# Layer 0's per-layer embedding product at the start of a two-layer encoder kernel, its bias table's product first, and the table's eight skewed copies written one per block

## The chip, the cores and the metric

The kernel runs on 1 core of one Trainium2 chip. The metric is device microseconds of one execution; the times shown are the median of 3 runs with their lowest and highest. The profile is of one further execution. The granted TensorE clock of that execution was 0.989 of full speed on average.

## The reference, cut to what matters

The kernel computes two encoder layers on 1024 tokens of width 1024 in float32. Layer 0 mixes tokens by neighbourhood attention (16 heads), layer 1 by differential attention (8 heads) with a bias from a table of 32 buckets. Each layer ends with a gated per-layer embedding; `p[i]` and `ple_w_proj[i]` are inputs that depend on nothing computed before.

```python
def reference(x, p, norm_g, ...):
    for i in range(DEPTH):
        h = rms_norm(x, g[0])
        m = neighborhood_attention(...) if i % 2 == 0 else diff_attention(..., t5_table)
        x = x + rms_norm(m, g[1])
        f = conv_glu_ffn(rms_norm(x, g[2]), ...)
        x = x + rms_norm(f, g[3])
        gate = jax.nn.sigmoid(rms_norm(x, g[4]) @ ple_w_gate[i])
        x = x + gate * (p[i] @ ple_w_proj[i])
    return x
# inside diff_attention, for query positions qpos of a block:
#   bias = t5_table[t5_bucket(kpos[None, :] - qpos[:, None])]
```

## The kernel before, in words

**Products.** Every float32 operand of the large products is split into a high and a low part: ScalarE copies the rounded high part (L85), VectorE subtracts it from the source (L86). `mm3` (L104 to L109) then issues three matmuls of 128x128 by 128x512, high by high, high by low, low by high. `load_split` (L93) is the same with a load ahead of it into one of three `raw` pages.

**Order of the work.** PE's instructions stand in the order in which the program writes them. The other engines' order, and that of SP, whose queue issues every DMA, is set by the scheduler of the tile framework. Pages and banks are reused in turn; an instruction that needs a page waits for the last user of what lay there. SP's DMAs use eight completion lanes in turn: a DMA is issued only when the one eight places before it has landed.

**Start of layer 0.** `enter` (L1121) loads eight tiles of x, normalises each (square on ScalarE, L114, power on GpSimd, L119, product on VectorE, L127) and transposes them on PE (L135) into four `r1` pages, high and low parts for the two halves of the width. After four tiles it begins the first two projections on 256 columns (`begin`), and `mid` transposes the other four tiles between the steps of the queries' projection.

**Neighbourhood attention.** `qkv_stream` (L228) is a generator of projection steps, three matmuls each: for each of eight blocks of two heads the keys, the queries and the values. `na` (L441) runs 64 rounds of scores, softmax, transposes and values and takes some six steps of the generator in each round (`tick`). Block 0's projections run before the first round.

**Bias table of layer 1.** After block 0's queries `da_tables` (L480) multiplies the table of 32x8 by a one-hot matrix of 32x2047 in four matmuls (L491), writes the 8x2047 result to DRAM (L494) and issues eight DMAs from DRAM to DRAM (L500), each writing one head's row 128 times with a shift of one place, 1023.5 KB each. They are read in layer 1.

**Embedding product.** `embeddings` (L1099) splits the 256x1024 of p (transposed) and of `ple_w_proj`, and multiplies them: eight tiles of tokens, two halves, two steps of three matmuls, 96 matmuls of 512 columns; ScalarE copies each half to a page (L1118) and SP writes each tile to the DRAM tensor `pp` (L1119), which the end of the layer reads. Its 32 steps follow the last projection in the generator and so fill the last five rounds of attention, ahead of `first_out` (L651), which loads and splits the attention's output weight `na_w_o` and multiplies the first token tile by it (L637) in 14 steps. `mix_out` is the output stage that follows (L637 with `m`).

## Time and profile before

| | us |
|---|---|
| median of 3 runs (lowest, highest) | 2787.24 (2779.03, 2789.44) |
| profiled execution, its own time | 2781.16 |
| its span (first to last instruction) | 2779.2 |
| layer 0's embedding product, first to last matmul | 441.05 to 475.65 |
| the four matmuls of the bias table, first to the next product | 56.98 to 60.91 |
| the eight skewed copies, issue on SP | 64.11 to 69.24 |

A row of the timeline has the start in us, the length in us, the engine, the line, the operation, the tiles written and read (buffer numbers left out), their shapes, and in brackets the idle time of the engine before it with what ended it. A matmul's length holds its drain through the array, so the distance from one start to the next tells its pace. SPq is SP issuing DMAs; "DMA to landing" counts from the issue to the arrival. Of a table of stretches the columns are the stretch, its length, the busy time and count on PE, PE's weight loads, VectorE, ScalarE and GpSimd, the granted clock, the share of the 16 DMA engines that was busy, and GB/s.

### The profile page before, as it was taken

Reading aid. Unit: us, or ns where it says so; the run is one execution under the profiler, and the core shown is the slowest. Engines: PE = TensorE matmul, PEld = TensorE weight load, DVE = VectorE, ACT = ScalarE, POOL = GpSimd, SP = SyncE. Lnnn points to the kernel's source line nnn. Section 1 sums busy time; section 2 is a strip of 40 time slices with the busy share of each in tenths; the row PEclk is TensorE's granted clock in tenths of the full one; section 3 lists DMA queues with packets and bytes.
Section 4 is the critical chain, followed back from the end, with each engine's and each line's share of the span. In section 5 each row is a group of like instructions: output and inputs, shape, how many; then the busy total and the mean of one; then the engine's idle time right before and its main releaser. Section 6 shows DMA issues by size and latency. Waiting matters only on the chain.

```text
span 2779.2 us, 36486 instructions
## 1 busy us (share of the span) xinstructions
PE 2703.0 (97%) x13312; PEld 2257.8 (81%) x13312; DVE 1985.5 (71%) x3409; ACT 1344.3 (48%) x2491; POOL 498.3 (18%) x473
## 2 busy tenths in 40 slices
PE   7999999989999999999999999999989999999999
PEld 5788888867888888888888888887868888888887
DVE  5677776687777777666677777776687767777664
ACT  4555556443444435454455555566354444444452
POOL 2121220023334300001000000000033343300000
PEclk9999999999999999999999999999999999999999
DMA  6412214623222373343211111115413333272342
GB/s 183 169 52 67 64 49 158 166 71 106 106 96 104 108 266 117 106 143 115 98 45 45 45 46 45 38 38 179 138 64 114 103 103 114 94 285 93 116 149 98
DMA packets 129477, 298.48 MB, mean 107 GB/s; under 512 B 11753, under 2 KB 37737, under 8 KB 129297
## 3 DMA queue, kind: packets, MB, share of 16 engines
q1 hardware_dynamic: 129296, 296.15, 32.4%
q8 instruction: 104, 1.70, 0.3%
q14 instruction: 77, 0.62, 0.1%
HBM read 221.69 MB, written 86.61 MB: 111 GB/s over the span
## 4 chain that ended last, share of the span: by engine, by line
PE 87%; DMA 5%; DVE 4%; ACT 2%; issue 1%; POOL 0%; SPq 0%; ACTq 0%; DVEq 0%; POOLq 0%
PE b L107 20%; PE b L108 20%; PE b L109 20%; PE g L637 5%; PE m L637 5%; PE b L553 4%; PE s L515 2%; PE s L516 2%; PE b L539 2%; PE av L426 2%; PE b L135 2%; PE b L410 1%; DVE r L86 1%; DMA raw<-in_qkv 1%; DMA raw<-in_ple_w_gate 1%
## 5 line engine op out<-in xcount | busy, mean ns | idle before, releaser
L107 PE MATMUL b<-r,ws 128*128 128x512 f32 (+1 forms) x1328 | 549.3, 414 | 12.8 <-ACT r L85 9.5
L109 PE MATMUL b<-r,ws 128*128 128x512 f32 (+1 forms) x1328 | 521.0, 392 | 0.5 <-DVE ws L86 0.5
L108 PE MATMUL b<-r,ws 128*128 128x512 f32 (+1 forms) x1328 | 519.9, 391 | 1.0 <-DVE r L86 0.8
L107 PEld LDWEIGHTS b<-r,ws 128*128 128x128 f32 x1328 | 253.7, 191 | 59.4 <-ACT r L85 11.0
L109 PEld LDWEIGHTS b<-r,ws 128*128 128x128 f32 x1328 | 252.3, 190 | 54.0 <-DVE ws L86 1.0
L119 POOL TENSOR_TENSOR ss<-ss,mhalf 128x1 f32<-128x1 f32 x136 | 90.8, 669 | 1137.4 <-DVE ss L557 566.5
L368 ACT ACTIVATE E<-E,mn 128x1024 f32<-128x1024 f32 (+2 forms) x256 | 221.9, 867 | 147.5 <-DVE mn L364 145.1
L108 PEld LDWEIGHTS b<-r,ws 128*128 128x128 f32 x1328 | 254.2, 191 | 39.7 <-DVE r L86 3.3
L107 PE MATMUL b<-r,wa 128*128 128x512 f32 x688 | 268.6, 390 | 7.5 <-DVE v L906 7.5
L107 PE MATMUL b<-r,r 128*128 128x512 f32 x680 | 268.9, 395 | 4.0 <-DVE v L911 2.9
L108 PE MATMUL b<-r,wa 128*128 128x512 f32 x688 | 268.4, 390 | 0.0
L109 PE MATMUL b<-r,wa 128*128 128x512 f32 x688 | 268.3, 390 | 0.0
L109 PE MATMUL b<-r,r 128*128 128x512 f32 x680 | 265.2, 390 | 0.0
L108 PE MATMUL b<-r,r 128*128 128x512 f32 x680 | 265.2, 390 | 0.0
L86 DVE TENSOR_TENSOR r<-raw,r 128x512 fp32r<-128x512 f32 (+1 forms) x178 | 140.5, 795 | 110.9 <-ACT r L85 110.6
L85 ACT ACTIVATE r<-raw 128x512 fp32r<-128x512 f32 (+1 forms) x178 | 121.4, 689 | 198.7 <-PE b L108 161.6
L86 DVE TENSOR_TENSOR ws<-raw,ws 128x512 fp32r<-128x512 f32 (+3 forms) x168 | 157.6, 946 | 63.2 <-ACT ws L85 61.2
L85 ACT ACTIVATE ws<-raw 128x512 fp32r<-128x512 f32 (+3 forms) x168 | 124.6, 749 | 140.1 <-PE b L109 57.7
L364 DVE CUSTOM_DVE_ANT_0 E<-s,T 128x1024 f32<-128x1024 f32 x128 | 156.5, 1223 | 33.8 <-PE s L516 32.5
L107 PEld LDWEIGHTS b<-r,wa 128*128 128x128 f32 x688 | 129.7, 189 | 35.3 <-ACT cv L916 5.3
L637 PE MATMUL m<-r,ws 128*128 128x512 f32 x672 | 156.7, 392 | 0.0
L637 PE MATMUL g<-r,ws 128*128 128x512 f32 x672 | 155.9, 391 | 0.0
(182 smaller groups left out, 5336.4 us busy)
## 6 DMA issues: line engine op xcount, KB each, us to landing
raw<-in_w_in SPq DMA_DIRECT2D x86, 512.0 KB, 3.5
raw<-in_qkv SPq DMA_DIRECT2D x48, 512.0 KB, 5.6
spillS<-r SPq DMA_DIRECT2D x88, 256.0 KB, 2.7
r<-in_ffn_w_out SPq DMA_DIRECT2D x40, 512.0 KB, 10.1
raw<-spillS SPq DMA_DIRECT2D x40, 512.0 KB, 3.5
spillA<-cv SPq DMA_DIRECT2D x66, 256.0 KB, 2.6
raw<-spillA SPq DMA_DIRECT2D x30, 512.0 KB, 3.7
x<-x SPq DMA_DIRECT2D x24, 512.0 KB, 3.7
```

The lines of the kernel that those rows point to most:

```text
L85: nc.scalar.activation(hi, src, AF.Copy)
L86: nc.vector.tensor_tensor(out=lo, in0=src, in1=hi.bitcast(F32), op=ALU.subtract)
L107: mm(out, sta[0], mov[0], start=first, stop=False, skip_group_check=onto)
L108: mm(out, sta[0], mov[1], start=False, stop=False, skip_group_check=onto)
L109: mm(out, sta[1], mov[0], start=False, stop=last, skip_group_check=onto)
L119: self.nc.gpsimd.tensor_tensor(out=ss, in0=ss, in1=self.mhalf, op=ALU.pow)
L135: self.nc.tensor.transpose(t[:, k * P : k * P + P], h[:, c : c + P], self.ident)
L364: nc.vector.tensor_tensor_reduce(out=e, in0=s, in1=bias, scale=1.0, scalar=3e38, op0=ALU.add, op1=ALU.min, accum_out=mn)
L368: nc.scalar.activation(e, e, AF.Exp, bias=mn, scale=-1.0, accum_out=sm)
L426: nc.tensor.matmul(out, V[:, kb, m], a[:, at * P : (at + w) * P], start=i + z == 0, stop=i == len(steps) - 1 and z == 1)
L553: nc.tensor.matmul(o, wT[:, k], V[:, k], start=k == 0, stop=k == KT - 1)
L637: mm(out[half], a, b[:, w], start=first and k + z == 0, stop=last and k == n - 1 and z == 2)
```

## The change

Layer 0's embedding product goes to the start. `enter` takes the product's four loads ahead of x, splits them and runs the 32 steps while x arrives; from the twelfth step on it transposes one tile of x after every fourth step, and tiles 6 and 7 stay for `mid`. The product has four PSUM banks of its own (`pe`), and its results lie in a page `e` with two buffers; a quarter of the sixteen half tiles is copied by VectorE, the rest by ScalarE. The `begin` on 256 columns is gone. Layer 0's generator now ends with the values and `first_out`; layer 1's is as before. `da_tables` is called ahead of `enter`, with its one-hot matrix in two halves, and `da_skew(j)` issues one skewed copy in each block of layer 0's generator. No product or its arithmetic changes.

```diff
@@ -90,9 +90,9 @@
                 out=lo, in0=src, scalar=scale, in1=hi.bitcast(F32), op0=ALU.mult, op1=ALU.subtract
             )
 
-    def load_split(self, src, shape=(P, D), dst=None, scale=None):
-
-        raw = self.page(self.raw, "raw", shape)
+    def load_split(self, src, shape=(P, D), dst=None, scale=None, raw=None):
+
+        raw = self.page(self.raw, "raw", shape) if raw is None else raw
         self.nc.sync.dma_start(raw, src)
         if dst is None:
             hi, lo = self.page(self.ws, "ws", shape, F32R), self.page(self.ws, "ws", shape, F32R)
@@ -278,9 +278,10 @@
             if j > 0:
                 yield from queries(0)
             yield from queries(1)
-            if j == 0 and layer == 0:
-                self.da_tables()
-                self.lam()
+            if layer == 0:
+                self.da_skew(j)
+                if j == 0:
+                    self.lam()
             self.qk[j] = Q, KH, KL
             if j + 1 < KT:
                 wk = self.wblock(W[KT + j + 1])
@@ -305,8 +306,8 @@
                         self.v[2 * j] = v
                     yield
                 nc.scalar.activation(vT[:, tb * 512 : tb * 512 + 512], ps, AF.Copy)
-                if tb == 0 and j == KT - 1:
-                    emb = self.embeddings(layer)
+                if tb == 0 and j == KT - 1 and layer == 1:
+                    emb = self.embeddings(layer, self.pj)
                     next(emb)
             if j + 1 < KT:
                 wq = self.wblock(W[j + 1])
@@ -317,7 +318,8 @@
 
         yield
         values()
-        yield from emb
+        if layer == 1:
+            yield from emb
         yield from self.first_out(layer)
 
     def begin(self, stream):
@@ -480,25 +482,33 @@
     def da_tables(self):
 
         nc = self.nc
-        t = self.page(self.r2, "r2", (32, 2, 2048))
-        hot, f = t[:, 0, :FW], t[:D_HEADS, 1, :FW]
         tab = self.const.tile([32, D_HEADS], F32, tag="t5", name="t5")
         nc.sync.dma_start(tab, self.i["t5_table"])
-        nc.sync.dma_start(hot, self.i["c_onehot"])
-        for c in range(4):
-            s = slice(c * 512, min(c * 512 + 512, FW))
-            ps = self.bank()[:D_HEADS, : s.stop - s.start]
-            nc.tensor.matmul(ps, tab, hot[:, s], start=True, stop=True)
-            nc.scalar.activation(f[:, s], ps, AF.Copy)
+        hot = [self.page(self.ws, "ws", (32, 1024)) for _ in range(2)]
+        f = [self.page(self.ws, "ws", (D_HEADS, 1024)) for _ in range(2)]
         F = self.dram.tile([D_HEADS, FW], F32, tag="t5f", name="t5f")
-        nc.sync.dma_start(F, f)
+        for c in range(2):
+            n = min(1024, FW - c * 1024)
+            nc.sync.dma_start(hot[c][:, :n], self.i["c_onehot"][:, c * 1024 : c * 1024 + n])
+        for c in range(2):
+            n = min(1024, FW - c * 1024)
+            for k in range(0, n, 512):
+                s = slice(k, min(k + 512, n))
+                ps = self.bank()[:D_HEADS, : s.stop - s.start]
+                nc.tensor.matmul(ps, tab, hot[c][:, s], start=True, stop=True)
+                nc.scalar.activation(f[c][:, s], ps, AF.Copy)
+            nc.sync.dma_start(F[:, c * 1024 : c * 1024 + n], f[c][:, :n])
+        self.t5, self.skewed = F, []
+
+    def da_skew(self, h):
+
         W = FW + P
-        self.skewed = []
-        for h in range(D_HEADS):
-            R = self.dram.tile([P, W], F32, tag=f"t5s{h}", name=f"t5s{h}")
-            flat = R.rearrange("q w -> (q w)")
-            nc.sync.dma_start(bass.AP(flat.tensor, flat.offset, [[W + 1, P], [1, FW]]), F[h].partition_broadcast(P))
-            self.skewed.append(R)
+        R = self.dram.tile([P, W], F32, tag=f"t5s{h}", name=f"t5s{h}")
+        flat = R.rearrange("q w -> (q w)")
+        self.nc.sync.dma_start(
+            bass.AP(flat.tensor, flat.offset, [[W + 1, P], [1, FW]]), self.t5[h].partition_broadcast(P)
+        )
+        self.skewed.append(R)
 
     def da_scores(self, x, n, m):
         nc = self.nc
@@ -1096,7 +1106,7 @@
                     to_next(t - 1)
         yield hT, mid
 
-    def embeddings(self, layer):
+    def embeddings(self, layer, banks, x=None):
 
         nc = self.nc
         a = self.page(self.r2, "r2", (P, 2, 2, SEQ), F32R)
@@ -1104,48 +1114,61 @@
         for k in range(2):
             rows = slice(k * P, k * P + P)
             self.load_split(self.i["pT"][layer][rows], dst=(a[:, k, 0], a[:, k, 1]))
-            self.load_split(self.i["ple_w_proj"][layer][rows], dst=(b[:, k, 0], b[:, k, 1]))
+            raw = None if k == 0 or x is None else self.page(x, "w", bufs=1)
+            self.load_split(self.i["ple_w_proj"][layer][rows], dst=(b[:, k, 0], b[:, k, 1]), raw=raw)
         yield
+        halves = (slice(0, 512), slice(512, D))
+
+        def part(o, t, w, k):
+            s = slice(t * P, t * P + P)
+            self.mm3(o, (a[:, k, 0, s], a[:, k, 1, s]), (b[:, k, 0, w], b[:, k, 1, w]), k == 0, k == 1)
+
+        def copy(t, half, e, o):
+            if x is not None and half and t % 2 == 0:
+                nc.vector.tensor_copy(e[:, halves[half]], o)
+            else:
+                nc.scalar.activation(e[:, halves[half]], o, AF.Copy)
+
+        early = []
+        if x is not None:
+            early = [self.bank(banks) for _ in range(4)]
+            for n, o in enumerate(early):
+                part(o, n // 2, halves[n % 2], 0)
         for t in range(NT):
-            s = slice(t * P, t * P + P)
-            e = self.page(self.ws, "ws")
-            for half in range(2):
-                w = slice(half * 512, half * 512 + 512)
-                o = self.bank(self.pj)
+            e = self.page(self.ws, "ws") if x is None else self.page(x, "e", bufs=2)
+            for half, w in enumerate(halves):
+                o = early.pop(0) if early else None
                 for k in range(2):
-                    self.mm3(o, (a[:, k, 0, s], a[:, k, 1, s]), (b[:, k, 0, w], b[:, k, 1, w]), k == 0, k == 1)
+                    if o is None or k == 1:
+                        o = self.bank(banks) if o is None else o
+                        part(o, t, w, k)
                     yield
-                nc.scalar.activation(e[:, w], o, AF.Copy)
-            nc.sync.dma_start(self.pp[layer][s], e)
+                copy(t, half, e, o)
+            nc.sync.dma_start(self.pp[layer][t * P : t * P + P], e)
 
     def enter(self, hT):
 
         nc = self.nc
         hs = [self.page(self.r2, "r2", (P, 4, D)) for _ in range(2)]
-        with self.tc.tile_pool(name="xe", bufs=1, reuse_waits="tile") as x:
+        with self.tc.tile_pool(name="xe", bufs=1, reuse_waits="tile") as x, self.psum("e", 4) as pe:
             turn = lambda u, groups=(0, 1): self.transposed(hs[u // 4][:, u % 4], self.put_hT(hT, u), groups=groups)
-            begun = []
-
-            def begin(w):
-                ps = self.bank(self.pj)
-                self.project(w, hT, ps, 0, 0, 256)
-                begun.append((ps, 256))
-
+            emb = self.embeddings(0, pe, x)
+            next(emb)
             for t in range(NT):
                 xi = self.page(x, "x", bufs=NT)
                 nc.sync.dma_start(xi, self.rows_of(self.i["x"], t, True))
                 if t == 0:
                     g0 = self.bcast(x, "g0", self.i["norm_g"][0, 0])
-                h = hs[t // 4][:, t % 4]
-                self.normed(xi, h, g0)
-                if t == 1:
-                    wk, wq, _ = self.first_weights(0)
-                if t == 3:
-                    turn(0), turn(1), begin(wk), turn(2), begin(wq), turn(3)
-            first = wk, wq, begun
+                self.normed(xi, hs[t // 4][:, t % 4], g0)
+                if t == 4:
+                    first = self.first_weights(0)
+            for n, _ in enumerate(emb):
+                if n >= 11 and n % 4 == 3:
+                    turn((n - 11) // 4)
 
         def mid(k):
-            turn(4 + k // 2, (k % 2,))
+            if k < 4:
+                turn(6 + k // 2, (k % 2,))
 
         return first, mid
 
@@ -1159,6 +1182,7 @@
         spill = {k: self.scratch(f"spill{k}", (FT // 2, P, 512)) for k in ("A11", "A12", "A22", "S1", "S2", "S3", "S4")}
         hT = self.hT_pages(self.r1, "r1")
         self.constants()
+        self.da_tables()
         first, mid = self.enter(hT)
         self.late_constants()
         for n in range(2):
```

What the scheduler makes of it on SP, the order of DMAs. Before, from the write of the bias table's product (`t5f`) on; `t5s0` to `t5s7` are the skewed copies, and the three `raw` pages behind them weights of block 1 and 2:

```order
L494 DMA t5f_515<-r2_59_499 8x2047
L500 DMA t5s0_517<-t5f_515 128x2047
L500 DMA t5s1_519<-t5f_515 128x2047
L500 DMA t5s2_521<-t5f_515 128x2047
L500 DMA t5s3_523<-t5f_515 128x2047
L500 DMA t5s4_525<-t5f_515 128x2047
L500 DMA t5s5_527<-t5f_515 128x2047
L500 DMA t5s6_529<-t5f_515 128x2047
L500 DMA t5s7_531<-t5f_515 128x2047
L96 DMA raw_105_702<-in_qkv 128x1024
L96 DMA raw_148_902<-in_qkv 128x1024
L96 DMA raw_182_1072<-in_qkv 128x1024
```

Now, behind the loads of x; `pp0<-e` are the results of the embedding product, tile by tile:

```order
L1147 DMA pp0_87<-e_49_240 128x1024
L1147 DMA pp0_87<-e_50_250 128x1024
L172 DMA raw_98_642<-in_da_lambda 128x256
L508 DMA t5s0_640<-t5f_111 128x2047
L508 DMA t5s1_1181<-t5f_111 128x2047
L508 DMA t5s2_1742<-t5f_111 128x2047
L508 DMA t5s3_2303<-t5f_111 128x2047
L508 DMA t5s4_2864<-t5f_111 128x2047
L508 DMA t5s5_3425<-t5f_111 128x2047
L508 DMA t5s6_3986<-t5f_111 128x2047
L508 DMA t5s7_4547<-t5f_111 128x2047
L1147 DMA pp0_87<-e_51_260 128x1024
```

The eight copies are one row of DMAs in both; they moved from behind the product in block 0 to between the second and the third of the eight results. Behind the last row follow the fourth result, a weight block, the other four results, the attention's mask and the pages of its bias.

ScalarE at the same place, from the square of the last tile of x on (`r2_14` from `x_43`); `e` are copies of the product's banks `b1`, `r1` the transposed x. The lanes and engines that a row waits for stand in brackets:

```order
L114 ACTIVATE r2_14_129,ss_44_219<-x_43_217 128x1024 [waits DMAHW3_49,DVE_49]
L1130 ACTIVATE e_51_260<-b1_52_261 128x512 [waits DMAHW1_49,Activation_49]
L1130 ACTIVATE e_56_292<-b1_57_293 128x512 [waits DMAHW2_49,Activation_49]
L1130 ACTIVATE e_56_292<-b1_58_301 128x512
L181 ACTIVATE lams0_644<-lams0_644 128x1 [waits DVE_49]
L181 ACTIVATE lams1_648<-lams1_648 128x1 [waits DVE_49]
L85 ACTIVATE r1_1_97<-b1_64_340 128x4x128 [waits PE_49]
L85 ACTIVATE r1_2_98<-b1_65_347 128x4x128 [waits PE_49]
L85 ACTIVATE r1_1_97<-b1_69_372 128x4x128 [waits PE_49]
L85 ACTIVATE r1_2_98<-b1_70_379 128x4x128 [waits PE_49]
L1130 ACTIVATE e_61_324<-b1_62_325 128x512 [waits DMAHW4_49,Activation_49]
L1130 ACTIVATE e_66_356<-b1_67_357 128x512 [waits DMAHW5_49,Activation_49]
```

All of this is new at this place. DMAHW4 is the lane of the write of `e_51`, whose buffer `e_61` takes over; bank `b1_62` is taken over by tile 6's product.

PE at the end of layer 0's generator, from the transposes of the last values (`raw`) on. Before, with the embedding product (`r2` by `r2`) as the next step:

```order
L135 MATMUL b1_955_4627<-ident_101,raw_908_4426 128x128 x4
L107 MATMUL b1_957_4635<-r2_932_4521,r2_931_4520 128x512
L108 MATMUL b1_957_4635<-r2_932_4521,r2_931_4520 128x512
L109 MATMUL b1_957_4635<-r2_932_4521,r2_931_4520 128x512
L426 MATMUL av_958_4639<-Ahi_938_4542,r2_835_4063 128x256
```

Now, with the output weight's product (`r1` by `ws`):

```order
L135 MATMUL b1_983_4732<-ident_101,raw_942_4549 128x128 x4
L428 MATMUL av_1001_4783<-Ahi_966_4647,r2_869_4184 128x256
L428 MATMUL av_1001_4783<-Alo_967_4648,r2_869_4184 128x256
L428 MATMUL av_1001_4783<-Ahi_966_4647,r2_869_4184 128x256
L428 MATMUL av_1001_4783<-Alo_967_4648,r2_869_4184 128x256
L428 MATMUL av_1001_4783<-Ahi_966_4647,r2_869_4184 128x128
L428 MATMUL av_1001_4783<-Alo_967_4648,r2_869_4184 128x128
L647 MATMUL b1_999_4781<-r1_984_4739,ws_994_4765 128x512
L647 MATMUL b1_1000_4782<-r1_984_4739,ws_994_4765 128x512
L390 MATMUL s_1004_4794<-r2_868_4183 128x384
L391 MATMUL s_1004_4794<-r2_869_4184,r2_868_4183 128x384
L390 MATMUL s_1007_4803<-r2_868_4183 128x256
```

The output weight's first product stands where the embedding product stood, with the scores of the next round (L390) behind it.

## The prediction

> **What bounds the kernel now.** I read the page first, then the stretches of the first 60 us, then the rows of single instructions at the two places that the change touches.
>
> ```profile
> PE 2703.0 (97%) x13312; PEld 2257.8 (81%) x13312; DVE 1985.5 (71%) x3409; ACT 1344.3 (48%) x2491; POOL 498.3 (18%) x473
> ...
> PE 87%; DMA 5%; DVE 4%; ACT 2%; issue 1%; POOL 0%; SPq 0%; ACTq 0%; DVEq 0%; POOLq 0%
> ```
>
> PE is busy 97% of 2779.2 us and carries 87% of the chain that ended last. Moving PE work can only pay where PE idles, and the change moves it from the end of layer 0's attention to the start. Table of stretches (us, then PE, PEld, DVE, ACT, POOL busy, granted clock, DMA share, GB/s):
>
> ```profile
> 0.00:10.00 10.00, 0.45 (x2) 0.45 (x3) 1.50 (x3) 2.47 (x4) 0.76 (x5) 1.00 0.76 204
> 10.00:20.00 10.00, 6.84 (x29) 5.39 (x27) 7.13 (x11) 7.70 (x13) 2.43 (x3) 1.00 1.04 269
> 20.00:30.00 10.00, 6.19 (x49) 5.61 (x48) 7.07 (x13) 5.12 (x10) 5.18 (x5) 1.00 0.88 232
> 30.00:40.00 10.00, 8.90 (x50) 8.06 (x49) 4.48 (x12) 3.61 (x8) 2.45 (x4) 0.66 0.62 223
> 40.00:60.00 20.00, 18.77 (x94) 13.50 (x93) 11.40 (x15) 9.71 (x17) 8.87 (x12) 1.00 0.40 93
> ```
>
> PE idles 9.55 + 3.16 + 3.81 + 1.10 + 1.23 = 18.9 us of the first 60, while the DMA engines are nearly full. Arrival of x, ScalarE's first and last look at it, and the end of the start:
>
> ```profile
> 6.20 1.06 ACT L114 ACTIVATE r<-x 128x1024 f32<-128x1024 f32 x1 [4.19 <-DMA x<-in_x]
> ...
> 26.30 1.06 ACT L114 ACTIVATE r<-x 128x1024 f32<-128x1024 f32 x1 [1.16 <-DMA x<-in_x]
> ...
> 56.98 1.88 PE L491 MATMUL b<-r,t 32*8 32x512 f32 x4
> ...
> 60.91 0.50 PE L107 MATMUL b<-r,ws 128*128 128x512 f32 x1
> ```
>
> Ten blocks of 512 KB (g0, seven x, two weights) land between the first two rows: 2.01 us a block. At 60.91 block 0's queries and keys and the bias product are done; this is my mark.
>
> **The embedding product, moved forward.** Its first and last matmul before, two groups of three apart by one group, and two cold rows of 256 columns:
>
> ```profile
> 441.05 0.78 PE L107 MATMUL b<-r,r 128*128 128x512 f32 x1
> ...
> 451.31 0.39 PE L107 MATMUL b<-r,r 128*128 128x512 f32 x1
> ...
> 452.01 0.39 PE L107 MATMUL b<-r,r 128*128 128x512 f32 x1
> ...
> 475.65 0.39 PE L109 MATMUL b<-r,r 128*128 128x512 f32 x1
> ```
>
> Three matmuls take 0.70 us, one 0.233; 96 of them 22.4 us. If the 18.9 us of idle took them in, the start would cost some 4 us. It will not, because of the queue. The skewed copies before:
>
> ```profile
> 64.11 5.13 SPq L500 DMA_DIRECT2D t5s<-t5f  x8
> ...
> DMA to landing us min/median/max: 6.0/14.4/24.1
> ...
> 70.20 26.47 DMA raw<-in_qkv
> ```
>
> The eight copies of 1 MB are issued from 64.1 to 68.6; the first lands at 70.1, the last at 92.7, so 3.23 us each, one behind another. A weight block of 512 KB issued at 70.20 lands only 26.47 us later: what SP issues behind the copies lands behind them. After the change the order of SP has all eight copies in one row still, directly behind the first two results of the embedding product and ahead of the other six. Written one per block, they are hoisted, since nothing but a semaphore lane holds them.
>
> Step by step. Ahead of the last x stand four more blocks, two quarter blocks (one-hot) and a table of 64 KB: 4.6 x 2.01 = 9.3 us, so it lands at 35.5. Behind it come a weight block, two results and lambda, 3.25 blocks, to 42. The copies can be issued from 35.5 on (lambda waits for the lane of the last x) and drain 8 x 3.23 = 25.8 us later, at 68. The third result, one more block, lands at 70. Page e has two buffers, so ScalarE's copy of token tile 4 (its row `e_61_324<-b1_62_325` in the order above) waits for that landing. Behind it on ScalarE stand the other results, the transposed tiles and block 0's keys. Tile 6's product on PE waits for the bank that this copy frees, and the transposes of tiles 4 to 7 and all queries and keys stand behind tile 6. How PE gets there: its first product needs both inputs split, about 11 us; four banks hold tiles 0 and 1; tile 4's bank comes free with `e_51_260<-b1_52_261`, which stands on ScalarE behind the square of the last x, 35.5 + 1.2 = 36.7. Tiles 4 and 5 with a cold start and two tiles' transposes are done at about 45. Then PE stands still until 70.5, 25 us.
>
> From there to the mark: 24 + 96 matmuls x 0.233 = 28.0, eight groups of four transposes x 0.36 = 2.9 (38.49 to 38.85 in the rows below), 1 us of small waits, and a cold start:
>
> ```profile
> 30.84 0.58 PE L107 MATMUL b<-r,ws 128*128 128x256 f32 x1
> ...
> 33.41 0.41 PE L107 MATMUL b<-r,ws 128*128 128x256 f32 x1
> ...
> 34.05 0.41 PE L107 MATMUL b<-r,ws 128*128 128x256 f32 x1
> ...
> 37.46 0.28 PE L108 MATMUL b<-r,ws 128*128 128x256 f32 x1
> ...
> 38.49 0.60 PE L135 MATMUL b<-ident,r 128*128 128x128 f32 x4
> 38.85 0.36 PE L107 MATMUL b<-r,ws 128*128 128x256 f32 x1
> ```
>
> After a gap of 4 us PE ran at 0.213 a matmul of 256 columns from 30.84 to 37.3 and at 0.117 after it: 6.4 us at 55% lose 2.9. The Trainium skill, "TensorE: Matmul & The Clock Gate", Part 1, puts the slow stretch at about 3.4 us of sustained work; by it the loss would be 1.5 and the sum 1.4 us less at each cold start. The rows here are longer, and I keep 2.9.
>
> 70.5 + 28.0 + 2.9 + 1 + 2.9 = 105.3 against 60.9: **+44.4 us at the mark**. Bounds: copies at 2.7 us each (PE again at 66) and two blocks later (75), so +40 to +49. The 105.3 holds nothing of the bias product: its 3.9 us (56.98 to 60.91) lie ahead of 11 us now, under the arrival of the embedding's inputs. Were that cover gone, they would come back whole. The halved first projections end as well: 96 matmuls of 256 columns at 0.117 become 48 at 0.233, nothing. Four of the sixteen copies to e go to VectorE, which is busy 1.5 + 7.1 + 7.1 of the first 30 us: nothing.
>
> The attention mask and the zeroed skew pages now stand behind the eight results on SP. Their chain before, from the first zeros to the first head's bias:
>
> ```profile
> 32.36 0.33 SPq L454 DMA_DIRECT2D skew<-bias  x1
> ...
> 46.92 2.35 POOL L357 TENSOR_TENSOR bias<-mask,shift 128x384 f32<-128x384 f32 x3 [5.87 <-DMA shift<-skew]
> ```
>
> That is 16.9 us. The last result is issued after tiles 6 and 7, one of them cold, and its copy, at about 81, so the bias is there at 98, ahead of the first scores at 105: nothing, and 1 us for each us beyond 105.
>
> **The wait that goes.** The queue behind the copies cost PE something before, too:
>
> ```profile
> 94.00:96.00 2.00, 0.63 (x3) 0.18 (x1) 0.18 (x2) 0.00 (x0) 0.00 (x0) 1.00 0.93 373
> 96.00:98.00 2.00, 0.19 (x1) 0.19 (x2) 0.21 (x1) 1.30 (x2) 0.00 (x0) 1.00 1.03 419
> 98.00:100.00 2.00, 1.48 (x5) 0.85 (x5) 1.97 (x6) 2.00 (x5) 0.15 (x1) 0.72 0.36 141
> 100.00:102.00 2.00, 2.00 (x9) 1.60 (x7) 2.00 (x3) 0.98 (x3) 0.49 (x1) 0.50 0.29 60
> ```
>
> Idle 1.37 + 1.81 + 0.52 = 3.7, and 1.6 lost to the clock (0.72 and 0.50 of two us each). After the change the queries' weights are issued at about 107 on an empty queue and are wanted at about 137: **-5.3**.
>
> **What the tail gives back.** The last projection, the first output product, the start of the output stage, and the stretch:
>
> ```profile
> 437.61 0.40 PE L109 MATMUL b<-r,ws 128*128 128x512 f32 x1
> ...
> 475.88 0.40 PE L637 MATMUL b<-r,ws 128*128 128x512 f32 x1
> ...
> 490.53 11.04 PE L637 MATMUL m<-r,ws 128*128 128x512 f32 x48
> ...
> 438.00:490.00 52.00, 48.89 (x258) 41.27 (x258) 35.07 (x77) 36.06 (x71) 0.00 (x0) 0.97 0.61 202
> ```
>
> Before, 52.9 us lie between the first and third row, and the embedding matmuls fill the waits of the last softmax rounds while the output weights load. Without them the first output product stands right behind the last projection in PE's order, and it needs the sixth load of that stage.
>
> ```profile
> 428.06 0.34 PE L388 MATMUL s<-r 128*128 128x384 f32 x1
> ...
> 434.51 0.42 PE L388 MATMUL s<-r 128*128 128x384 f32 x1
> ...
> 431.23 0.42 DVE L393 TENSOR_SCALAR E<-E,sum 128x384 f32<-128x384 f32 x1
> ...
> 432.84 1.23 DVE L86 TENSOR_TENSOR r<-raw,r 128x1024 fp32r<-128x1024 f32 x1 [0.39 <-ACT r L85]
> ...
> 453.98 1.06 ACT L85 ACTIVATE r<-raw 128x1024 fp32r<-128x1024 f32 x1
> ...
> raw<-in_w_in SPq DMA_DIRECT2D x86, 512.0 KB, 3.5
> ```
>
> A load takes 3.5 + 1.06 + 1.23 = 5.8 us from issue to free buffer, and there are three buffers. The sixth follows the third, which follows the first, whose page comes free some 4 us ahead of the end of the projections: 9 us after that end. Then two rounds of attention with their eighteen output matmuls, 6.45 each (428.06 to 434.51): 12.9; the cold start 2.9; six matmuls 1.4; three rounds with nothing between, each as long as its softmax (428.06 to 431.65) and its transposes, 4.3: 13; the last values and the split of the last head 7. Together 46: **-6.7**. Bounds: VectorE's 35.1 us of work, -17.8, and no gain, 0. I take the middle since every step but the loads is a chain of two engines.
>
> **Sum:** +44.4 - 5.3 - 6.7 = +32.4 us. The profiled execution took 2781.2 (span 2779.2), so 2813.6; against the median of 2787.2 that is 2819. A difference of over 0.5% (14 us) can be told from no change in this kernel.
>
> **Rivals.**
> 1. The tail gives all that VectorE allows: -17.8 in place of -6.7. For it: W_o's loads can begin before the projections end. Against it: PE's fixed order. +21.3, 2808, slower still.
> 2. The results do not queue behind the copies: the third lands about 48, PE goes on at 48, +22 at the mark, +10 in all, 2797, within 0.5%. For it: no row shows a write to DRAM behind these copies, only loads. Against it: the row of 26.47 us. The Trainium skill, "DMA: Bandwidth & Descriptors", Queues, rings and completion order, says a later descriptor may finish its write first but the completion count lands after all earlier writes of its engine; by that this rival has no time of its own.
> 3. Faster: the start runs at PE's own pace. Place: the two buffers of e and the four banks; it decides if each result lands within about 7 us of its issue and ScalarE copies a bank before PE wants it again. Price: PE from 11 us on without a gap needs 22.4 + 22.4 (products, projections) + 5.8 (sixteen groups) + 2.9 + 1, so 65.5, +4.6 in place of +44.4, and -7.4 in all; with over 13.3 of the 17.8 in the tail it is faster by over 0.5%, with all of it -18.5, 2769. For it: 18.9 us of idle are there. Against it: two orders, SP's and ScalarE's.
>
> **How the numbers follow.** Forecast 0.64, rival 1 0.19, rival 2 0.12, rival 3 0.05. The first two are slower by over 0.5%; with 0.01 of rival 2, whose late copies could lift it over 14 us, that is 0.84. Within 0.5% lie the rest of rival 2 and the 0.01 of rival 3 with a short tail: 0.12. Faster is 0.04. The range goes from rival 2 (2796) to the forecast with late copies and no gain in the tail (+44.4 + 4.6 = +49, 2836).
>
> **What would show it.** In the profile after: PE idle for some 25 us between 45 and 70, ended by ScalarE's copy to e; t5s issued at about 36 and the third pp landing 20 us or more after its issue; no wait at the queries of block 1; the output stage of layer 0 about 46 us behind the last projection, with a wait of 6 us at its first product. I am wrong if pp lands within 6 us beside the copies, or if PE has no gap over 10 us before the mark.

## The result and the profile after

The changed kernel takes 2802.15 us in the median of five runs (2800.02 to 2806.36), the kernel before 2786.76 in five runs beside them: a ratio of 1.0065, with an interval from 1.0054 to 1.0076. The profiled execution took 2800.02 us with a span of 2798.2, against 2781.16 and 2779.2, so 19.0 us of span are to be found. I had forecast 2819 and slower. It is slower, but by less: 15.4 us between the medians and 19.0 between the profiled spans, where my sum had +32.4. The two profiled executions lie some 3.5 us further apart than the medians; the stages below add up to the 19.0.

In the rows PE is TensorE and PEld its weight loads, DVE is VectorE, ACT is ScalarE, POOL is GpSimd. The table of stretches of the changed kernel (us, then PE, PEld, DVE, ACT, POOL busy, granted clock, DMA share, GB/s):

```profile
30.00:40.00 10.00, 2.89 (x9) 2.17 (x8) 7.41 (x14) 5.07 (x11) 3.34 (x4) 0.67 1.03 311
40.00:50.00 10.00, 7.79 (x35) 6.21 (x34) 2.91 (x7) 2.52 (x6) 0.00 (x0) 0.82 1.02 312
50.00:60.00 10.00, 0.00 (x0) 0.00 (x0) 0.00 (x0) 0.00 (x0) 0.00 (x0) 0.52 0.86 272
60.00:70.00 10.00, 0.00 (x0) 0.00 (x0) 0.34 (x1) 0.28 (x1) 0.00 (x0) 0.50 0.82 313
```

From 50 to 70 us PE does nothing and the other engines work for 0.6 us together, while the DMA engines are over 80% busy. What they move and who waits for it stands in the chain of waits (start, length, what; a DMA's length runs to its landing, and the second row is the third result's):

```profile
33.72 9.52 DMA t5s<-t5f
43.31 26.33 DMA pp<-e
69.72 0.61 ACT e L1130
70.37 0.80 PE b L107
```

The copies are issued from 33.72 on, the third result at 43.31; it lands 26.33 us later, ScalarE's copy into its buffer of e follows, and PE goes on at 70.37. The list of PE's waits up to 520 us (in total, times, longest) has that stop as the longest, and the wait at the first output product as the next:

```profile
PE b L107 <- ACT e L1130: 31.5, 3, 22.6
PE b L647 <- ACT ws L85: 6.6, 1, 6.6
```

PE's rows: the product of tile 4, with a shorter stop ahead of it; then the end of the start (before: 60.91), the last projection (437.61), the first output product, and the output stage (490.53):

```profile
37.40 0.80 PE L107 MATMUL b<-r,r 128*128 128x512 f32 x1 [7.11 <-ACT e L1130]
...
103.30 0.39 PE L107 MATMUL b<-r,ws 128*128 128x512 f32 x1
...
472.67 0.40 PE L109 MATMUL b<-r,ws 128*128 128x512 f32 x1
...
482.34 1.22 PE L647 MATMUL b<-r,ws 128*128 128x512 f32 x2 [6.61 <-ACT ws L85]
...
512.24 11.18 PE L647 MATMUL m<-r,ws 128*128 128x512 f32 x48
```

I had forecast the shorter stop by ScalarE's order: bank free at 36.7, behind the square of the last x. The time is right and the cause isn't. ScalarE's row of the copy that frees the bank waits 2.25 us more, for the first result to land, so the two buffers of e set this stop as well:

```profile
36.75 0.60 ACT L1130 ACTIVATE e<-b 128x512 f32<-128x512 f32 x1 [2.25 <-DMA pp<-e]
```

The start became 103.30 - 60.91 = 42.4 us longer. From there to the last projection lie 369.37 us in place of 376.70: 7.3 less. From the last projection to the output stage lie 39.57 in place of 52.92: 13.35 less. From there to the end lie 2285.96 in place of 2288.67: 2.7 less. Together 42.4 - 7.3 - 13.35 - 2.7 = 19.05, the whole difference of the spans.

### The profile page after: what moved, and what is told of

It reads as the page before. It is cut to its first block, busy times and chain, and to the rows that moved or that the text cites. A ratio compares the mean times of both kernels' runs of the same rounds, so it can differ in the third digit from the quotient of the medians.

```text
span 2798.2 us, 36405 instructions
## 1 busy us (share of the span) xinstructions
PE 2701.7 (97%) x13264; PEld 2252.1 (80%) x13264; DVE 1988.3 (71%) x3413; ACT 1340.9 (48%) x2487; POOL 496.6 (18%) x473
## 4 chain that ended last, share of the span: by engine, by line
PE 87%; DMA 5%; DVE 4%; ACT 1%; issue 1%; POOL 0%; SPq 0%; DVEq 0%; ACTq 0%; POOLq 0%
PE b L107 20%; PE b L108 20%; PE b L109 20%; PE g L647 5%; PE m L647 5%; PE b L563 4%; PE s L525 2%; PE s L526 2%; PE b L549 2%; PE b L135 2%; PE av L428 2%; PE b L412 1%; DVE r L86 1%; DMA x<-in_x 1%; DMA pp<-e 1%
## 5 line engine op out<-in xcount | busy, mean ns | idle before, releaser
L107 PE MATMUL b<-r,ws 128*128 128x512 f32 x1312 | 543.1, 414 | 9.5 <-ACT r L85 9.5
L109 PE MATMUL b<-r,ws 128*128 128x512 f32 x1312 | 515.6, 393 | 0.0
L108 PE MATMUL b<-r,ws 128*128 128x512 f32 x1312 | 514.6, 392 | 0.0
L107 PEld LDWEIGHTS b<-r,ws 128*128 128x128 f32 x1312 | 248.2, 189 | 54.6 <-ACT r L85 10.3
L109 PEld LDWEIGHTS b<-r,ws 128*128 128x128 f32 x1312 | 247.2, 188 | 53.7
L108 PEld LDWEIGHTS b<-r,ws 128*128 128x128 f32 x1312 | 248.9, 190 | 38.4 <-DVE r L86 1.2
L86 DVE TENSOR_TENSOR ws<-raw,ws 128x512 fp32r<-128x512 f32 (+3 forms) x168 | 156.9, 942 | 56.1 <-ACT ws L85 54.6
L107 PEld LDWEIGHTS b<-r,r 128*128 128x128 f32 x680 | 129.3, 190 | 67.8 <-ACT e L1130 32.3
```

Source lines behind the costliest of these rows:

```text
L86: nc.vector.tensor_tensor(out=lo, in0=src, in1=hi.bitcast(F32), op=ALU.subtract)
L107: mm(out, sta[0], mov[0], start=first, stop=False, skip_group_check=onto)
L108: mm(out, sta[0], mov[1], start=False, stop=False, skip_group_check=onto)
L109: mm(out, sta[1], mov[0], start=False, stop=last, skip_group_check=onto)
```

## The experiments

The theory: the third result stands behind the eight copies in SP's queue; with two buffers of e and four banks ScalarE and then PE stop for it. Against it: ScalarE's order and the arrival of x set the stop; or it is the DMA engines that are full, whatever the queue. All kernels in one table, from PE's rows of each profiled run (us): the start of the first scores, from there to the last projection, on to the output stage, on to the end of the span; then the median and the ratio to runs of the kernel before beside it. The median of these runs was 2785.1 beside e1 to e4, 2782.8 beside e5 to e8 and 2784.7 beside e9 to e12, so kernels of different groups are compared by their ratios.

| kernel | first scores | to last projection | to output stage | to the end | median | ratio (interval) |
|---|---|---|---|---|---|---|
| before | 62.02 | 375.6 | 52.9 | 2288.7 | 2786.8 | |
| after | 103.98 | 368.7 | 39.6 | 2286.0 | 2802.2 | 1.0065 (1.0054 to 1.0076) |
| e1 tables back | 80.19 | 375.4 | 39.6 | 2284.5 | 2787.4 | 1.0007 (0.9997 to 1.0016) |
| e2 tables alone | 59.53 | 380.2 | 54.6 | 2291.8 | 2785.6 | 1.0007 (0.9997 to 1.0017) |
| e3 e in x | 76.81 | 379.9 | 41.1 | 2287.3 | 2785.5 | 1.0000 (0.9991 to 1.0009) |
| e4 half the copies | 87.84 | 368.7 | 40.4 | 2285.5 | 2784.9 | 0.9997 (0.9987 to 1.0006) |
| e5 own queue | 94.80 | 368.7 | 39.2 | 2285.6 | 2793.6 | 1.0038 (1.0026 to 1.0049) |
| e6 own queue, e in x | 86.56 | 379.6 | 39.8 | 2286.2 | 2793.7 | 1.0037 (1.0024 to 1.0051) |
| e7 held | 73.74 | 373.1 | 39.0 | 2285.2 | 2777.0 | 0.9976 (0.9966 to 0.9986) |
| e8 held, later product | 74.82 | 373.8 | 37.8 | 2286.7 | 2773.7 | 0.9968 (0.9957 to 0.9979) |
| e9 one per block | 75.88 | 370.8 | 39.5 | 2286.2 | 2776.1 | 0.9971 (0.9960 to 0.9981) |
| e10 one per block, two e | 78.25 | 370.8 | 39.5 | 2289.2 | 2780.1 | 0.9986 (0.9977 to 0.9994) |
| e11 tables held alone | 58.85 | 372.9 | 53.0 | 2290.1 | 2777.1 | 0.9977 (0.9968 to 0.9986) |
| e12 one per block, later product | 74.96 | 370.8 | 37.5 | 2286.6 | 2772.2 | 0.9957 (0.9945 to 0.9970) |

**e1, the bias table back in its old place.**

```diff
-        self.da_tables()
...
-            if layer == 0:
-                self.da_skew(j)
-                if j == 0:
-                    self.lam()
+            if j == 0 and layer == 0:
+                self.da_tables()
+                self.lam()
```

with the old da_tables and its loop over the eight copies.

> The embedding product stays at the start; the bias table's product and all eight skewed copies go back to where the kernel before had them, behind block 0's queries. Theory (the copies stand ahead of the third result in SP's queue, two buffers of e then stop ScalarE and PE): the third result lands 3 to 6 us after its issue in place of 26.3, PE's stop of 22.6 us between the transposes of tile 3 and tile 6's product shrinks to under 5, block 0's queries end near 84 in place of 103, the wait for block 1's queries comes back with 4 to 5 us, about 2787 us in all. Rival (PE stops there because of ScalarE's order and the arrival of x, the copies are beside it): the stop stays over 15 us, 2802 or more, and the bias product's 4 us and the wait of 5 on top.

Measured: 2787.4. The list of PE's waits has one for ScalarE's copies to e and again one at block 1's queries:

```profile
PE b L107 <- ACT e L1121: 6.2, 1, 6.2
PE b L107 <- ACT ws L85: 3.0, 1, 3.0
```

The view of the results pp, from issue to landing:

```profile
DMA to landing us min/median/max: 2.7/3.6/6.5
```

None takes more than 6.5 us now, where the third took 26.3. The stop of 22.6 is gone wholly; the 6.2 are at 35.24, at tile 4's product, where the changed kernel has its 7.1. The first scores start 24 us earlier, with the bias product's 4 ahead of them. So the long stop goes with the copies, and the shorter one does not.

**e2, the bias table alone.**

```diff
 (the kernel before)
+        self.da_tables()
...
-            if j == 0 and layer == 0:
-                self.da_tables()
-                self.lam()
+            if layer == 0:
+                self.da_skew(j)
+                if j == 0:
+                    self.lam()
```

with the new da_tables and da_skew.

> The other part alone: the bias table's product ahead of all and its copies one per block, with layer 0's embedding product left where the kernel before had it. Theory: the copies are hoisted here too, but no product waits for what stands behind them, except the attention mask and the zeroed skew pages; 3.9 us of bias product and 5.3 us at block 1's queries go, and the first head's bias comes late by 0 to 15 us: 2778 to 2793 us, with no stop of PE over 15 us. Rival (a hoisted burst costs PE some 22 us whatever stands behind it): 2800 or more.

Measured: 2785.6, in the expected span. SP's rows show the four zeroings of the attention's pages behind the burst, some 4 us one after another:

```profile
34.54 0.47 SPq L507 DMA_DIRECT2D t5s<-t5f  x1
37.87 0.33 SPq L455 DMA_DIRECT2D skew<-bias  x1
...
49.79 0.32 SPq L456 DMA_DIRECT2D skew<-bias  x1
```

What it cost is in PE's list of waits, at the second group of scores (73.22). It waits for VectorE to take the first group's scores, and these wait for their bias:

```profile
PE s L389 <- DVE mn L365: 8.8, 1, 8.8
```

So each part alone costs nothing net that can be measured (+0.07% both; in e2 the gains at the bias product and at block 1's queries are spent at these scores), and the two together cost 0.65%: the price lies in their meeting.

**e3, no result is waited for.**

```diff
-            e = self.page(self.ws, "ws") if x is None else self.page(x, "e", bufs=2)
+            e = self.page(self.ws, "ws") if x is None else self.page(x, "x", bufs=NT)
```

> The changed kernel with one thing altered: the embedding product's results go into the eight pages of x, which are free by then, in place of two buffers of e, so that no copy waits for a result to land. The burst stays where it is. Theory: PE's stop of 22.6 us and the clock's slow start behind it go, block 0's queries end near 78 to 80, and the first head's bias (mask and skew pages still behind the copies) may come up to 7 us late: 2777 to 2785 us. Rival (ScalarE's order and the arrival set the stop): 22.6 stays, 2802.

Measured: 2785.5, at the upper end of the theory's range. The stop of 22.6 is gone though the burst starts at much the same time (35.8 us in place of 33.7) and results still take up to 19.8 us to land: nothing waits for them. Two more results go out ahead of the burst here, so this run changes more than the buffers. At the second group of scores PE waits 9.2 us where I expected up to 7, and GpSimd's rows and PE's say why:

```profile
75.12 0.61 POOL L253 CAST r<-r 64x512 fp32r<-64x512 f32 x1
76.60 0.85 POOL L452 MEMSET bias<- 128x896 f32 x1 [0.87 <-DMA pp<-x]
88.69 2.30 POOL L359 TENSOR_TENSOR bias<-mask,shift 128x384 f32<-128x384 f32 x3 [11.24 <-DMA shift<-skew]
...
90.84 0.69 PE L390 MATMUL s<-r 128*128 128x384 f32 x1 [9.16 <-DVE mn L366]
```

The zero page is made only at 76.60, behind the casts of block 0's keys on GpSimd, which end at 75.73, and then the landing of a result, which frees the memory 0.87 us later. The pages, the shift and the bias follow. So SP's queue is the last step here, as I had it, but without it GpSimd's order would have held the page nearly as long.

**e4, half the copies.**

```diff
     def da_skew(self, h):
+        if h % 2:
+            self.skewed.append(self.skewed[-1])
+            return
```

> The changed kernel with four of the eight skewed copies left out (odd heads of layer 1 read the copy of the even head ahead of them, so layer 1's bias is another there). Theory: four copies at 3.23 us fewer ahead of the third result, so PE's stop falls from 22.6 to about 10 us and the time to about 2789. Rival (the stop is not the copies'): it stays above 20 us and the time at 2802.

Measured: 2784.9, some 4 us under the expected 2789. The third result in the chain of waits, and PE's stop ahead of tile 6's product:

```profile
37.10 16.12 DMA pp<-e
...
53.95 0.80 PE L107 MATMUL b<-r,r 128*128 128x512 f32 x1 [7.32 <-ACT e L1133]
```

The result lands at 53.22 in place of 69.64, 16.4 us earlier for four copies, 4.1 each where I had 3.23 from before. PE's stop falls by 22.59 - 7.32 = 15.3 us. The stop follows the dose; a stop of ScalarE's own order would not.

**e5 and e6, the copies on a queue of their own.**

```diff
-        self.nc.sync.dma_start(
+        self.nc.scalar.dma_start(
             bass.AP(flat.tensor, flat.offset, [[W + 1, P], [1, FW]]), self.t5[h].partition_broadcast(P)
```

> The changed kernel with the eight skewed copies issued by ScalarE, so on another DMA queue than the results, at about the same time (33 to 45 us); nothing else altered. Theory (the results are held back by their place in SP's queue): the third result shares the engines with the copies but does not stand behind them, lands within 12 us of its issue in place of 26.3, PE's stop falls from 22.6 to under 8, the time to about 2786. Rival (the DMA engines are full for 26 us with 8 MB, whatever queue it comes from): the third result still lands 20 us or more after its issue, and the time stays at 2798 to 2802.

> The copies on ScalarE's queue and the results in the pages of x. What was left in the run with the results in x alone was 9.2 us at the first scores, for the attention mask and skew pages behind the copies. Theory (place in SP's queue): that wait falls under 3 us, 2776 us. Rival (full engines): it stays at 7 us or more, 2783 to 2785.

Measured for e5: 2793.6, between the two. SP's row of the third result's issue and ScalarE's row of the copy that waits for its landing:

```profile
44.85 0.32 SPq L1147 DMA_DIRECT2D pp<-e  x1
...
54.98 0.60 ACT L1130 ACTIVATE e<-b 128x512 f32<-128x512 f32 x1 [5.95 <-DMA pp<-e]
```

The chain of waits has a copy and the fourth result:

```profile
35.77 16.51 DMA t5s<-t5f
52.34 11.81 DMA pp<-e
```

The list of PE's waits:

```profile
PE b L107 <- ACT e L1130: 21.4, 4, 8.0
```

The third result takes some 10.1 us (44.85 to 54.98) beside the copies on another queue, within the 12 that the theory gave it, and 26.3 behind them on its own; no result takes over 6.5 with no copies about (e1). So some 16 us of the 26.3 are the place in the queue, and the shared engines add 4 to 7 to the 2.7 to 6.5 of e1. The fourth result still takes 11.8. Of PE's four waits the 8.0 is the shorter stop ahead of tile 4; the long one is split into 7.3, 3.4 and less. The total is 7 us over the theory's 2786. The copies still hold SP, whose issues wait for a lane: in the chain the fourth result's issue at 52.34 follows the landing of a copy issued at 35.77. In e6 the wait at the second group of scores stayed at 8.1, the rival's side, but the total lies above both expectations. ScalarE's rows, the copies' issues (ACTq) among them, and one of GpSimd:

```profile
49.89 0.48 ACTq L508 DMA_DIRECT2D t5s<-t5f  x1
50.41 0.60 ACT L85 ACTIVATE r<-b 128x512 fp32r<-128x512 f32 x1 [8.56 <-DMA pp<-x]
...
85.42 0.84 POOL L452 MEMSET bias<- 128x896 f32 x1
```

The seventh copy's issue waits for a result's landing, and ScalarE's split of the transposed x behind it stands for 8.56 us, PE with it (8.5). And the zero page is made at 85.42, behind GpSimd's casts, so the wait of 8.1 is the order on GpSimd; the run can't tell the queue from the engines there.

**e7 and e11, the copies held, with and without the embedding's move.** The last 127 columns of the bias product wait for block 0:

```diff
+        last = c.tile([32, 127], F32, tag="hot3", name="hot3")
...
+        def rest():
+            product(last[:D_HEADS], last)
+            nc.sync.dma_start(F[:, 1920:FW], last[:D_HEADS])
...
             if layer == 0:
+                if j == 0:
+                    self.t5_rest()
                 self.da_skew(j)
```

e7 has e in the pages of x too; e11 puts the same into the kernel before.

> The results in the pages of x, and the copies truly held: the last 127 columns of the bias table's product are left to block 0, behind its queries, so that no copy can be issued before about 77 us; the other 1920 columns stay ahead of all. Theory: no result, mask or skew page stands behind a copy, so PE has no stop over 4 us between the first embedding product and the first scores, the 9.2 us of the run with the results in x alone are gone, block 1's queries wait up to 4 us; 2774 to 2778 us, some 10 under the kernel before. Rival (a stop of this size comes back elsewhere, for block 1's weights behind the copies): 2783 or more.

> The kernel before with the bias table's product ahead of all and the copies held behind block 0's queries; layer 0's embedding product stays at the end of the attention. It tells what the embedding product's place is worth by itself, against the held kernel. Theory: 3.9 us of bias product leave PE's path (0.3 come back), the wait for block 1's queries stays: 2779 to 2781 us, so the embedding product's move is worth 3 to 6 us once nothing stands ahead of its results. Rival (the embedding product at the start is worth nothing even then): 2777 or less.

Measured: e7 2777.0, e11 2777.1. In e7 GpSimd makes the zero page early and SP issues the copies late:

```profile
48.42 0.85 POOL L454 MEMSET bias<- 128x896 f32 x1 [10.96 <-DMA pp<-x]
...
77.08 4.69 SPq L519 DMA_DIRECT2D t5s<-t5f  x7
```

Of PE's waits up to 520 us the longest are at the first output product, for the one-hot pages at the very start, for the split of a transposed x, and, fifth, for block 1's weights:

```profile
PE b L658 <- ACT ws L85: 6.5, 1, 6.5
PE b L500 <- DMA ws<-in_c_onehot: 4.3, 1, 4.3
PE b L135 <- DVE r L86: 3.8, 1, 3.8
...
PE b L107 <- ACT ws L85: 2.3, 1, 2.3
```

So e7 is as the theory had it. Against e11 it says what the embedding's move is worth when nothing stands ahead of its results: the start is 73.74 - 58.85 = 14.9 us longer, the end of the attention 14.0 shorter; the spans differ by 3.8 us (2771.0 and 2774.8), the ratios not at all (0.9976 and 0.9977). The 3.8 us are not the move's: in the stretch behind the output stage the two profiled executions differ by 4.9, and e7's is the fastest of its nine. I had expected 3 to 6 us; the rival was right. The gain of e7 over the kernel before can be had from the bias table alone.

**e8, the first output product one round later.** In the held kernel:

```diff
-        yield
+        for _ in range(1 if layer else 7):
+            yield
         yield from self.times_steps(m, [(hi[:, k], lo[:, k]) for k in range(KT - 1)], self.W[: KT - 1], last=False)
```

> The held kernel with the first output product of layer 0 put one round of attention later in TensorE's fixed order, so that a round of attention stands where TensorE waits 6.6 us for the loads of the output weights. Theory (the stretch is set by TensorE's order and the loads, VectorE is not the end of it): that wait falls to 3 us or less, the stretch from the last projection to the output stage from 39.6 to about 36, 3 to 4 us under the held kernel. Rival (VectorE's softmax chain sets the stretch, the wait only hides under it): the stretch stays within 1 us of 39.6 and the two kernels agree.

Measured: 2773.7. The wait and its place:

```profile
459.91 0.80 PE L658 MATMUL b<-r,ws 128*128 128x512 f32 x1 [4.23 <-ACT ws L85]
```

It falls from 6.5 to 4.2 (expected 3 or less), since the loads' splits now stand behind the softmax on ScalarE and the product starts 11.3 us after the last projection in place of 9.5. The stretch falls from 39.0 to 37.8, 1.2 us where the theory had some 3.6: nearer to the rival. The medians lie 3.3 us apart, as the theory had it, but the intervals of e7 and e8 overlap.

**e9, e10 and e12, one copy per block.** Each block makes the last 64 columns of its own head:

```diff
+    def t5_rest(self, h):
+        tab, last = self.t5_last
+        row = self.const.tile([1, 64], F32, tag="row3", name=self.uid("row3"))
+        ps = self.bank()[:1, :64]
+        nc.tensor.matmul(ps, tab[:, h : h + 1], last, start=True, stop=True)
+        nc.scalar.activation(row, ps, AF.Copy)
+        nc.sync.dma_start(self.t5[h : h + 1, FW - 64 : FW], row)
...
             if layer == 0:
+                self.t5_rest(j)
                 self.da_skew(j)
```

e9 has e in x, e10 the two buffers of the change, e12 is e9 with the later product of e8.

> The change as its words say it: the results in the pages of x, and each skewed copy truly held to its block (the last 64 columns of the bias table are made one head per block, behind that block's queries, and a head's copy needs its own). Theory (a queue's burst is the cost, one copy of 3.2 us among a block's loads is hidden): against the held kernel the wait of 2.3 to 3.3 us for block 1's weights goes, no other wait comes; 2771 to 2775 us. Rival (that wait comes from something else than the burst): it stays, and eight small products and copies more cost 1 to 2 us: 2777 or more.

> Each copy held to its block as in the run before, but the results in two buffers of e as the change has them. Theory (the two buffers only cost when a result lands late): with nothing ahead in the queue the third result lands 3 to 6 us after its issue, PE waits 6 to 10 us in all for ScalarE's copies to e as in the run with the tables put back, 2779 to 2783 us. Rival (the two buffers are harmless without the burst): within 2 us of the run with the pages of x.

> Each copy held to its block, results in the pages of x, and layer 0's first output product one round of attention later. Theory (the wait of 6.5 us there is only partly on the path): 0.5 to 2 us under the kernel with each copy held to its block. Rival (a full 4 us): 4 us or more under it.

Measured: 2776.1, 2780.1 and 2772.2. e9 lies between its theory (2771 to 2775) and its rival (2777 or more). Its copies land in 6.6 us each and PE waits nowhere between the first scores and the last projection: that stretch falls by 2.3 us against e7, the size of the wait for block 1's weights, as the theory had it. The total doesn't follow, since the first scores start 2.1 us later (75.88 in place of 73.74); in the start PE waits 2.1 us for ScalarE's copies to x, where e7 has 0.7. Why ScalarE's order came out otherwise there I did not follow up. In e10 PE waits 4.6 us for ScalarE's copies to e (expected 6 to 10):

```profile
PE b L107 <- ACT e L1143: 4.6, 2, 4.2
```

and it is 4 us above e9, as the theory had it (2779 to 2783). Of these the first scores account for 2.4, so the two buffers cost a little without a burst as well; the rest lies behind the output stage, where the kernels differ without a cause that I know. e12's stretch is 37.5 against 39.45 in e9, 2.0 less, as the theory had it, and its first scores are 0.9 earlier; the medians are 4 apart, the rival's size, and the intervals overlap, so the two can't be told apart. It is the fastest here: 0.9957 (0.9945 to 0.9970) of the kernel before.

## Why the direction was right and the size too large

| step | forecast | measured |
|---|---|---|
| third result lands | 70 | 69.6 |
| PE goes on | 70.5 | 70.37 |
| end of the start | +44.4 | +42.4 |
| middle of the attention | -5.3 | -7.3 |
| last projection to output stage | -6.7 | -13.35 |
| from there on | 0 | -2.7 |
| sum | +32.4 | +19.0 |

**The stop** was right in place and cause, and nearly in size (22.6 us, forecast 25). That it is the burst ahead of the results is shown by taking the burst away (e1), halving it (e4) and, with the order on SP a little changed, taking the buffers' dependence on it away (e3). Of my rivals the second (results don't queue behind copies) is refuted by the row of 26.33 us and, with e5, by the 10.1 us that the same result takes on a queue without the copies ahead of it. The Trainium skill, "DMA: Bandwidth & Descriptors", Queues, rings and completion order, by which the completion count lands after the earlier writes of its DMA engine, agrees with the row of 26.33 us.

**The cold start** behind the stop I put at 2.9 us. Nine matmuls at the slow pace, from the row of 70.37 above to

```profile
73.95 0.56 PE L109 MATMUL b<-r,r 128*128 128x512 f32 x1
74.34 0.39 PE L107 MATMUL b<-r,r 128*128 128x512 f32 x1
```

are 3.97 us in place of 9 x 0.233 = 2.1: 1.9 lost. I had kept 2.9 from the rows of before, so this term was 1 us too large. My other value, an estimate of 1.5 from the some 3.4 us of slow work that the Trainium skill, "TensorE: Matmul & The Clock Gate", Part 1, states, lies nearer to the 1.9 measured. With the waits of 1 us that didn't come, this is the 2 us at the mark.

**The middle** gave 2 us more, because I had overlooked a slow clock in the kernel before, behind its bias product:

```profile
60.00:62.00 2.00, 2.00 (x6) 0.93 (x5) 0.69 (x1) 1.63 (x3) 0.00 (x0) 0.83 0.25 72
62.00:64.00 2.00, 2.00 (x8) 1.78 (x7) 1.04 (x5) 0.67 (x3) 0.00 (x0) 0.50 0.28 33
64.00:66.00 2.00, 2.00 (x9) 1.61 (x8) 1.06 (x4) 0.64 (x2) 0.00 (x0) 0.81 0.01 4
```

2 x (0.17 + 0.50 + 0.19) = 1.7 us, at most 0.3 of it ahead of the mark at 60.91. So the bias product costs 3.9 us and some 1.7 of clock where it stood.

**The tail** is the step that failed, half of the error. I had: 9 us to the first output product, 12.9 + 2.9 for two rounds with output matmuls and the cold start, "three rounds with nothing between, each as long as its softmax (428.06 to 431.65) and its transposes, 4.3: 13; the last values and the split of the last head 7". The rows after show 482.34 - 473.07 = 9.3 for the first, and for the rest

```profile
498.42 1.09 PE L647 MATMUL b<-r,ws 128*128 128x512 f32 x4
...
500.53 0.39 PE L390 MATMUL s<-r 128*128 128x384 f32 x1
...
502.84 0.39 PE L390 MATMUL s<-r 128*128 128x384 f32 x1
...
505.46 1.20 PE L412 MATMUL b<-ident,E 128*128 128x128 f32 x6 [1.82 <-DVE sum L394]
...
510.62 1.61 PE L647 MATMUL b<-r,ws 128*128 128x512 f32 x6
```

The two rounds end at 499.51, 17.2 us after their start (15.8 forecast). From there to the last six output matmuls lie 11.1 us in place of 13 + 7. The scores of the last two rounds stand 2.3 us apart, ahead of the transposes of the round before: the rounds overlap. I used the latency of one round's chain where the distance from round to round counts. Rival 1, that the tail gives all that VectorE allows (-17.8), came out nearer than the forecast, though not for its reason, since VectorE isn't busy throughout:

```profile
473.00:512.20 39.20, 28.96 (x164) 24.40 (x163) 30.08 (x75) 23.84 (x52) 0.00 (x0) 0.87 0.50 159
```

30.1 of 39.2 us, and e8 and e12 still shorten the stretch by 1.2 and 2.0 us.

**After the tail** 1.3 us are a wait of PE at the transposes of h that before has and the changed kernel hasn't; the other 1.4 us I have not traced. In the table of kernels this stretch goes from 2284.5 to 2291.8, so the 2.7 may be no more than its scatter.

**Rival 3**, a start at PE's own pace, needed +4.6 us at the mark. Even with each result free to land (e7 against e11) the start is 14.9 us longer: of the 22.4 us of product the idle start hides only 7.5. I take the reason to be that PE's idle time there is time in which x arrives and is split, and that the product's inputs (2 MB) come ahead of x in the same queue; no run tries it.

## What to carry to other kernels

Work that is moved into an idle stretch brings its DMAs along: look at what stands ahead of them in the queue, and at how many buffers wait for their landing, before counting the idle time as free. A transfer that only a semaphore lane holds is not tied to the block in whose code it stands; a true dependence (here 64 columns made per block) ties it. And a tail of overlapping rounds is summed by the distance from round to round, not by the latency of one.

## What the runs showed of the hardware

The eight copies of 1 MB from DRAM to DRAM delay the transfer behind them on the same queue by 4.1 us each (e4: with four fewer it lands 16.4 us earlier). A transfer on another queue still takes up to 11.8 us beside them (e5), against 6.5 without (e1). An engine that issues DMAs can be held by them: ScalarE stood for 8.56 us behind one issue (e6). Behind the bias product's four matmuls (32 rows by 8 columns, 512 wide) the granted clock is 0.50 in a stretch of 2 us though PE stands still for no more than 0.25 us near it, in the kernel before (62 to 64 us) and in e1 alike:

```profile
80.00:82.00 2.00, 2.00 (x7) 1.81 (x7) 0.93 (x4) 0.58 (x3) 0.00 (x0) 0.50 0.32 42
```

At the same place in the changed kernel, where the product stands elsewhere, the clock is whole:

```profile
104.00:106.00 2.00, 2.00 (x12) 1.74 (x11) 1.48 (x3) 1.53 (x4) 0.82 (x2) 1.00 0.20 75
```

The nearest trial is e11, the kernel before with all but 127 of the 2047 columns taken away from this place. There the clock is whole too, behind a rest of the product that PE does in 0.38 us:

```profile
60.00:62.00 2.00, 2.00 (x11) 1.62 (x10) 1.88 (x7) 1.37 (x4) 0.00 (x0) 1.00 0.29 87
```

So the slow clock goes with the product; what it is about these matmuls that brings it, no run here shows.
